# A streaming-encoder layer on one Trainium2 core: the output projection in three phases of block pairs, its weights requested a tile ahead, and the first operands of the up- and down-projection made in the stage before

## The chip, the cores and the metric

The kernel runs on one core of one Trainium2 chip. The core has five instruction queues that work side by side and meet through semaphores: TensorE (PE in the profile, with PEld for its weight loads), VectorE (DVE), ScalarE (ACT), GpSimd (POOL) and SyncE (SP). In this kernel every transfer between the chip's memory (DRAM) and the core's buffer (SBUF) is issued from SP, and 16 DMA engines carry it out. The metric is the device time of one execution in microseconds (us), the median of the runs shown.

## What is computed

The reference is one step of a hybrid encoder layer, cut here to what the change touches. 2048 prompt frames and 64 frames of a running stream are laid side by side as 2112 columns.

```
x = x + mixed @ w_out                    # output projection, 1024 x 1024
xn2 = rmsnorm(x, norm_ffn)
up = xn2 @ w_up                          # 1024 x 5632
up_c, _ = causal_dwconv(up, fbuf, ffn_conv_w, ffn_conv_b)
gate, val = split(up_c, 2)
x = x + (silu(gate) * val) @ w_down      # 2816 x 1024
y = rmsnorm(x, norm_final)
```

Ahead of it lie the input projection, a gated linear recurrence and a windowed attention, which make `mixed`. They aren't changed.

## The kernel before, in words

All activations stand transposed: features on the 128 partitions, frames along the columns. A float32 product is made of three matmuls in a rounded format: an operand is split into a high part (ScalarE, a copy that rounds) and a low part (the difference, on VectorE or GpSimd), and the three are high by high, high by low, low by high. The helper `split` (L188) issues both halves, so that all high parts have line L190 and all low parts L191.

The 2112 columns form three pairs of blocks (`PAIRS`): two blocks of 320, two of 320, two of 416.

**Output projection** (`wout`, L752; matmuls L216 to L218). It runs in four phases: the first pair, the second pair, and the two blocks of 416 as a phase each. A phase goes through eight weight tiles m. In the first phase `kept` loads a tile raw, splits it and stores the split tile of 1 MiB to DRAM (`woS`); the later phases load that (L201), into two buffers. For each tile and block, 24 matmuls fill a PSUM bank, VectorE adds half of the result to the residual (L766), which was loaded from `xT` (L762) into one of two `xres` buffers, the sum is stored to `x1S` (L767), and its square is added to a running sum (L773, L774). Beside the weight tiles a list of generators is driven five steps at a time: `mixes` loads and splits the next phase's input (L754), and `xprep` makes the operands of the up-projection from `x1S` (L722 to L736). Those are seven for each pair: "11", "21", "22" and four sums and differences "T1" to "T4", since the up- and the down-projection multiply by a scheme of seven products instead of eight. After each phase `rms` makes 1/sqrt(mean square) for its blocks (matmul L674, square root L675, reciprocal L676).

**Up-projection** (`Lane`; matmuls L897 to L899). The list `plan` holds steps of one product each. 20 groups of weights serve pair 0 and pair 1 together (two lanes), two groups serve each alone, and then 11 steps with two groups each serve pair 2. Weights are loaded raw (`wraw`), combined (L850), split, and for later use stored to `wuS`. At the first step for pair 1 alone, pair 0's operands are given up and `xprep` begins for pair 2, from `x1S`.

**Down-projection** (matmuls L1191 to L1193). Seven products; in each, every pair goes through 11 weight tiles k, which serve four PSUM banks. `dweight` loads and combines weights (`draw`), four `dw` buffers hold them raw; `dtoken` loads and splits the up-projection's result from `hS`. In the second product a weight tile needs three raw tiles, and the combination is stored to `s2S` (L1117). Finished quarters get their residual and squares (`finished`), and `outputs` scales and stores them.

Memory is handed out by hand: `Region` is a stretch of SBUF, `Pool` gives slots of it by name, in turn, and a slot's next use waits for its last one. `acc` deals out eight PSUM banks in turn. The order on each queue follows the program's text only roughly: a scheduler in the framework places instructions by its own estimates and keeps their dependences. A queue works strictly in order, so what stands behind a waiting instruction waits too.

Of the kernel before, what the change touches and what calls it, by code (L numbers as in the profile page):

```python
# [7 lines left out]
F32 = mybir.dt.float32  # L8
# [43 lines left out]
class Region:  # L52
# [11 lines left out]
    def take(self, n):  # L64
        edges = [(0, 0)] + sorted(self.taken) + [(self.size, self.size)]
        for (_, a), (b, _) in zip(edges, edges[1:]):
            if b - a >= n:
                self.taken.append((a, a + n))
                return self, (a, a + n)
        return None  # L70
# [13 lines left out]
def take(regions, n):  # L84
    n = -(-n // 8) * 8
    for r in regions:
        got = r.take(n)
        if got:
            return got
    raise AssertionError(f"{4 * n} bytes asked for; taken: {[[(4 * a, 4 * b) for a, b in sorted(r.taken)] for r in regions]}")  # L90


class Pool:


    def __init__(self, *regions):
        self.regions, self.slots, self.turn = regions, {}, {}

    def reserve(self, name, n, bufs=1):
        self.slots[name] = [take(self.regions, n) for _ in range(bufs)]  # L100
        self.turn[name] = 0
# [19 lines left out]
def kernel(ctx: ExitStack, tc: tile.TileContext, xT, w_in, w_out, w_up, w_dn, gw, pk,  # L121
# [588 lines left out]

    def xprep(p, names, rs, tp):
# [4 lines left out]
        sums = "T2" in names  # L716
        for k in range(4):
            x = {}
            for o, kk, t in (("11", k, t0), ("12", k, t1), ("21", k + 4, t0), ("22", k + 4, t1)):
                if sums or o in names:  # L720
# [7 lines left out]
            if sums:  # L728
                t2 = tp.tile([P, n], F32, name="xt")
                nc.vector.tensor_tensor(x["11"], x["12"], x["11"], op=ALU.subtract)  # L730
                nc.vector.tensor_tensor(t2, x["22"], x["11"], op=ALU.subtract)
                nc.vector.tensor_tensor(x["12"], x["22"], x["12"], op=ALU.subtract)
                put(p, "T1", k, x["11"])
                put(p, "T2", k, t2)
                yield
                nc.vector.tensor_tensor(t2, x["21"], t2, op=ALU.subtract)  # L736
                put(p, "T3", k, x["12"])
# [3 lines left out]
    wpool, wp2, tp = Pool(RB), Pool(FW), Pool(FW)  # L741
    rawpool = Pool(FW)
    rsum = {}
    phases = [PAIRS[0], PAIRS[1], PAIRS[2][:1], PAIRS[2][1:]]
    mixp = [Pool(RA), Pool(RE), Pool(RE), Pool(RC)]

    def mixes(i):

        for t0, n in phases[i]:
            xblocks[t0] = tuple(mixp[i].tile([P, KO, n], F32R, name=f"{c}{t0}") for c in "hl")  # L750
            hi, lo = xblocks[t0]
            for k in range(KO):  # L752
                mr = wp2.tile([P, BM], F32, name="xk", bufs=2)[:, :n]
                nc.sync.dma_start(mr, mixS[k, :, t0:t0 + n])  # L754
                split(hi[:, k, :n], lo[:, k, :n], mr, nc.gpsimd if k % 3 == 1 and i < 2 else nc.vector)
                yield

    def wout(i, m):
        w = kept(m, i, True)
        for t0, n in phases[i]:  # L760
            xr = wp2.tile([P, BM], F32, name="xres", bufs=2)[:, :n]
# [3 lines left out]
            mm3(ps, w, hi, lo, n)  # L765
            nc.vector.scalar_tensor_tensor(xr, ps[:, :n], 0.5, xr, op0=ALU.mult, op1=ALU.add)  # L766
            nc.sync.dma_start(x1S[m, :, t0:t0 + n], xr)  # L767
            if m == 0:
                rsum[t0] = wp2.tile([P, BM], F32, name="rs", bufs=4)[:, :n]
                nc.scalar.activation(rsum[t0], xr, AF.Square)  # L770
            else:
                q = wp2.tile([P, BM], F32, name="sq", bufs=1)[:, :n]
# [13 lines left out]
    for name, b in (("xk", 2), ("xres", 2), ("rs", 4), ("sq", 1)):  # L786
        wp2.reserve(name, BM, b)
    beside = [mixes(0)]
    drive(beside, 99)
    for i, blocks in enumerate(phases):  # L790
        if i == 1:
            rawpool.close()
            wpool.close()
            wpool = Pool(RE)
            beside.append(xprep(0, ORDER, rsum, tp))
        if i == 2:
            beside.append(xprep(1, ("T1", "T2", "T3", "T4"), rsum, tp))
        if i == 3:
            beside.append(xprep(1, ("11", "21", "22"), rsum, tp))
        if i + 1 < len(phases):  # L800
            beside.insert(0, mixes(i + 1))
        if i == 1:
            wpool.reserve("whl", 2 * KO * P, 2)
        for m in range(8):
            wout(i, m)
            drive(beside, 5)
        drive(beside, 99)
        mixp[i].close()
        for t0, n in blocks:
            rms(rsum[t0], n, rsum[t0])  # L810
            if i > 1:
                nc.sync.dma_start(rS[:, t0:t0 + n], rsum[t0])
    tp.close()
    wp2.close()
    wpool.close()
    RC.close()
    FA = Region(tc, "FA", 26624, F32)
# [3 lines left out]
    wr, wh = Pool(FW), Pool(RE)  # L821

    def wraw(g, o, nb=6):

        t = wr.tile([P, 4 * P], F32, name="wr", bufs=nb)
# [5 lines left out]
    def wops(g, fresh, nh):  # L831
# [3 lines left out]
        def parts(src):  # L835
            t = wh.tile([P, 2, 4 * P], F32R, name="wh", bufs=nh)
# [3 lines left out]
        def kept_s(i, src):  # L840
# [3 lines left out]
            else:  # L844
                t = wh.tile([P, 2, 4 * P], F32R, name="wh", bufs=nh)
# [23 lines left out]
    def flush(i):  # L869
# [5 lines left out]
    class Lane:  # L875
# [48 lines left out]
        def conv_a(self, G, m):  # L924
            self.carry(G, m)
            uc = up["c"].tile([P, self.cols], F32, name="uc", bufs=4)
# [90 lines left out]
    wr.reserve("wr", 4 * P, 6)  # L1017
    up["s"], up["c"] = Pool(FA), Pool(FW, FA)
    up["c"].reserve("uc", 640, 4)
    x2 = []  # L1020

    def prepare(i):
# [3 lines left out]
        for g in dict.fromkeys(g for g, _ in lanes):  # L1026
            if u == 0:
                gens[g] = wops(g, fresh, 4)
# [3 lines left out]
    ahead, made = 3, 0  # L1032
    live = []
    for i, (lanes, fresh, u) in enumerate(plan):
        while made <= i:
            prepare(made)
            made += 1
        if u == 0:
# [312 lines left out]
```

## Time and profile before

| | us |
|---|---|
| median of 3 runs | 3093.64 |
| lowest and highest | 3085.44 and 3097.01 |
| the profiled execution's own time | 3103.43 |
| its span, first to last instruction | 3101.7 |
| PE busy, PEld busy | 2913.0 and 2824.1 |
| DVE, ACT, POOL busy | 2158.4, 1511.6, 168.4 |

The mean granted TensorE clock is 0.967 of full speed. DMA moved 587.06 MB, 189 GB/s over the span. By the first and last matmuls of each line, the input projection with recurrence and attention runs to about 1372 us of the span, the output projection from there to 1662.9, the up-projection to 2607.9 and the down-projection to the end. A row of a group of instructions names its line, engine, operation and tiles (written tile, arrow, read tiles), the shape, the count, busy time and mean duration in ns, and then the idle time ahead of it with what ended that. A row of waits names who waited for whom, the total in us, how often, and the longest. A row by stretches gives, for each engine, its busy us and number of instructions, then the mean granted clock, the mean busy share of the DMA engines and GB/s.

### The profile page before, as it was taken

How to read it: one execution, taken by the hardware profiler on the slowest of the kernel's cores; microseconds unless marked ns; L12 is line 12 of the kernel's file. 1: busy time of each engine (PE TensorE's matmuls, PEld its weight loads, DVE VectorE, ACT ScalarE, POOL GpSimd, SP SyncE). 2: the span in 40 equal slices, each digit the busy share in tenths (PEclk: the TensorE clock that was granted, in tenths of full speed). 3: DMA queues.
4: the chain of work that ended last, by engine and by line, in shares of the span. 5: the costliest groups of instructions: out<-in, count | busy, mean ns of one | idle time of the engine just before them, and what ended most of it. 6: DMA issues, size and time to landing. Idle time of an engine off the chain costs nothing.

```text
span 3101.7 us, 48466 instructions
## 1 busy us (share of the span) xinstructions
PE 2913.0 (94%) x17572; PEld 2824.1 (91%) x17572; DVE 2158.4 (70%) x4176; ACT 1511.6 (49%) x3404; POOL 168.4 (5%) x121
## 2 busy tenths in 40 slices
PE   8999999999999999987878999999799999899997
PEld 7988889999999999976868999999689999899997
DVE  5498882587883588863664888888876677466776
ACT  4576652466561466643323555555444444233442
POOL 3221212000000000002000000000000000000000
PEclk9999999999999999998989999999899999999999
DMA  7865537444336544436775555454776677675764
GB/s 254 284 217 188 182 136 240 154 134 136 126 117 200 165 136 135 137 130 224 253 232 204 176 184 181 164 177 169 265 230 229 227 229 226 196 216 177 223 191 129
DMA packets 338751, 587.06 MB, mean 189 GB/s; under 512 B 34928, under 2 KB 261680, under 8 KB 317520
## 3 DMA queue, kind: packets, MB, share of 16 engines
q1 hardware_dynamic: 338512, 583.97, 57.6%
q8 instruction: 138, 2.26, 0.3%
q14 instruction: 101, 0.83, 0.1%
HBM read 399.19 MB, written 185.18 MB: 188 GB/s over the span
## 4 chain that ended last, share of the span: by engine, by line
PE 43%; DMA 7%; DVE 3%; ACT 1%; issue 1%; SPq 0%; POOL 0%; DVEq 0%; ACTq 0%; POOLq 0%
PE mf L897 6%; PE mf L898 6%; PE mf L899 6%; PE mm L897 3%; PE mm L899 3%; PE mm L898 3%; PE mf L1192 3%; PE mf L1193 3%; PE mf L1191 3%; PE mm L1191 2%; PE mm L1193 2%; PE mm L1192 1%; DMA RE<-woS 1%; DMA FW<-in_w_dn_dram 1%; DMA FW<-mixS 1%; DMA x1S<-FW 1%
## 5 line engine op out<-in xcount | busy, mean ns | idle before, releaser
L216 PE MATMUL mm<-xh,whl 128*128 128x320 f32 (+2 forms) x2112 | 690.5, 327 | 9.7 <-ACT xh L190 6.3
L217 PE MATMUL mm<-xl,whl 128*128 128x320 f32 (+2 forms) x2112 | 688.6, 326 | 8.5 <-DVE xl L191 4.5
L218 PE MATMUL mm<-xh,whl 128*128 128x320 f32 (+2 forms) x2112 | 685.9, 325 | 0.0
L190 ACT ACTIVATE RE<-FW 128x512 fp32r<-128x512 f32 (+2 forms) x586 | 319.2, 562 | 450.3 <-PE mf L1193 74.0
L191 DVE TENSOR_TENSOR RE<-FW,RE 128x512 fp32r<-128x512 f32 (+2 forms) x580 | 345.0, 610 | 162.0 <-ACT RE L190 147.0
L216 PEld LDWEIGHTS mm<-xh,whl 128*128 128x128 f32 x2112 | 402.3, 191 | 17.3 <-ACT xh L190 8.7
L217 PEld LDWEIGHTS mm<-xl,whl 128*128 128x128 f32 x2112 | 401.5, 190 | 17.7 <-DVE xl L191 7.9
L218 PEld LDWEIGHTS mm<-xh,whl 128*128 128x128 f32 x2112 | 401.4, 190 | 0.8
L1192 PE MATMUL mf<-RE 128*128 128x320 f32 (+1 forms) x583 | 190.4, 327 | 5.4 <-DVE RE L191 5.4
L1191 PE MATMUL mf<-RE 128*128 128x320 f32 (+1 forms) x583 | 191.3, 329 | 0.0
L1193 PE MATMUL mf<-RE 128*128 128x320 f32 (+1 forms) x583 | 189.7, 325 | 0.0
L897 PE MATMUL mf<-RE 128*128 128x320 f32 (+1 forms) x472 | 154.8, 330 | 12.2 <-ACT RE L190 9.3
L933 DVE SCALAR_TENSOR_TENSOR FW<-FA,pkt,FW 128x640 f32<-128x640 f32 x176 | 154.7, 879 | 12.0 <-ACT FW L927 8.8
L898 PE MATMUL mf<-RE 128*128 128x320 f32 (+1 forms) x472 | 155.0, 328 | 0.6 <-DVE RE L191 0.6
L899 PE MATMUL mf<-RE 128*128 128x320 f32 (+1 forms) x472 | 154.4, 327 | 0.0
L897 PE MATMUL mm<-RE 128*128 128x320 f32 (+1 forms) x408 | 133.3, 327 | 6.6 <-DMA RE<-wuS 5.7
L897 PE MATMUL mf<-RA,RE 128*128 128x320 f32 (+1 forms) x416 | 137.2, 330 | 0.9 <-ACT FA L944 0.5
L899 PE MATMUL mm<-RE 128*128 128x320 f32 (+1 forms) x408 | 132.1, 324 | 5.4 <-DVE RE L191 5.4
L898 PE MATMUL mf<-RA,RE 128*128 128x320 f32 (+1 forms) x416 | 136.1, 327 | 0.0
L899 PE MATMUL mf<-RA,RE 128*128 128x320 f32 (+1 forms) x416 | 135.9, 327 | 0.2 <-DVE RE L191 0.2
L898 PE MATMUL mm<-RE 128*128 128x320 f32 (+1 forms) x408 | 132.3, 324 | 0.0
L447 ACT ACTIVATE pr<-S,nm 128x256 f32<-128x256 f32 (+1 forms) x272 | 123.3, 472 | 7.6 <-DVE nm L443 6.0
(329 smaller groups left out, 7121.2 us busy)
## 6 DMA issues: line engine op xcount, KB each, us to landing
whl<-wiS SPq DMA_DIRECT2D x88, 1024.0 KB, 5.1
RE<-wuS SPq DMA_DIRECT2D x96, 512.0 KB, 4.4
wiS<-whl SPq DMA_DIRECT2D x44, 1024.0 KB, 4.8
wuS<-RE SPq DMA_DIRECT2D x88, 512.0 KB, 2.7
FW<-in_w_up_dram SPq DMA_DIRECT2D x160, 256.0 KB, 3.4
FW<-in_w_dn_dram SPq DMA_DIRECT2D x121, 256.0 KB, 3.8
hS<-FA SPq DMA_DIRECT2D x154, 160.0 KB, 3.0
FW<-hS SPq DMA_DIRECT2D x154, 160.0 KB, 3.4
```

Source lines behind the costliest of these rows:

```text
L190: nc.scalar.activation(hi, src, AF.Copy)
L191: (lo_eng or nc.vector).tensor_tensor(lo, src, hi.bitcast(F32), op=ALU.subtract)
L216: nc.tensor.matmul(ps[:, :n], wh[:, c], xh[:, k, :n], start=first, stop=False)
L217: nc.tensor.matmul(ps[:, :n], wh[:, c], xl[:, k, :n], start=False, stop=False)
L218: nc.tensor.matmul(ps[:, :n], wl[:, c], xh[:, k, :n], start=False, stop=last)
L897: nc.tensor.matmul(ps[:, :n], w[:, 0, c], x[:, k, 0], start=first, stop=False, **more)
L898: nc.tensor.matmul(ps[:, :n], w[:, 0, c], x[:, k, 1], start=False, stop=False, **more)
L899: nc.tensor.matmul(ps[:, :n], w[:, 1, c], x[:, k, 0], start=False, stop=last, **more)
L933: nc.vector.scalar_tensor_tensor(uc, G[:, j:j + self.cols], col("fw", 44 * j + m), uc, op0=ALU.mult, op1=ALU.add)
L1191: nc.tensor.matmul(ps[m][:, :n], w[:, 0, c], t[:, 0], start=k == 0, stop=False)
L1192: nc.tensor.matmul(ps[m][:, :n], w[:, 0, c], t[:, 1], start=False, stop=False)
L1193: nc.tensor.matmul(ps[m][:, :n], w[:, 1, c], t[:, 0], start=False, stop=k == 10)
```

## The change

The output projection now has three phases, one for each pair. `wout` requests the tile of weights that follows (`wload`) directly behind its own matmuls, ahead of its residual, and the stores of a tile's sums are held in a list and issued one tile later, behind that request. The split weights of the first phase are stored from the same list. Raw weights come in two halves, and all low parts are made on VectorE. Four `xres` buffers stand in place of two. The norm of a phase is made behind the first tile of the next; that of pair 2 only at the first step for pair 1 alone in the up-projection, from sums stored raw in `rS`. `xprep` takes any subset of operands. Pair 0's are made in the second phase, of pair 1 "11", "T3", "T2", "T4" in the third, and "T1", "21", "22" beside the first four steps of the up-projection. The first weights of the up-projection are made within the last tile of the output projection; the first weights and two token tiles of the down-projection within the last four steps of the up-projection. The down-projection's raw weights use six buffers. The adding of residuals is separated from squares and done earlier, and the last product goes through pair 2, pair 1 and then pair 0 twice, with two banks each time.

The SP queue in the stretch of the output projection where blocks of 416 are worked, before (`woS` is the split weights, `x1S` the sums, `xT` the residual):

```order
L201 DMA RE<-woS 128x2048
L762 DMA FW<-in_xT_dram 128x416
L767 DMA x1S<-FW 128x416
L722 DMA FW<-x1S 128x320 x2
L201 DMA RE<-woS 128x2048
L722 DMA FW<-x1S 128x320 x2
L762 DMA FW<-in_xT_dram 128x416
L767 DMA x1S<-FW 128x416
L201 DMA RE<-woS 128x2048
```

and now:

```order
L780 DMA RE<-woS 128x2048
L812 DMA x1S<-FW 128x416
L733 DMA FW<-x1S 128x320 x2
L812 DMA x1S<-FW 128x416
L796 DMA FW<-in_xT_dram 128x416 x2
L733 DMA FW<-x1S 128x320
L780 DMA RE<-woS 128x2048
```

Between two weight tiles stood one residual and one store; now two of each stand there, since a tile serves both blocks.

The VectorE queue at the start of the up-projection, now (L734 scales a loaded tile of `x1S`, L740 forms T1, L198 makes low parts, L866 combines weights; FA is the stretch of memory that holds pair 1's raw tiles):

```order
L734 SCALAR_TENSOR_TENSOR FA<-FA,pkt,FW 128x320 x3
L740 TENSOR_TENSOR FA<-FA 128x320
L198 TENSOR_TENSOR RE<-FW,RE 128x512
L198 TENSOR_TENSOR RE<-FA,RE 128x320 x2
L734 SCALAR_TENSOR_TENSOR FA<-FA,pkt,FW 128x320
L198 TENSOR_TENSOR RE<-FW,RE 128x512
L866 TENSOR_TENSOR FW<-FW 128x512
L734 SCALAR_TENSOR_TENSOR FA<-FA,pkt,FW 128x320 x2
L740 TENSOR_TENSOR FA<-FA 128x320
L734 SCALAR_TENSOR_TENSOR FA<-FA,pkt,FW 128x320
L198 TENSOR_TENSOR RE<-FA,RE 128x320 x2
```

Before, this place held the up-projection's own weights and results alone; the operands of pair 1 had been made in the output projection.

The VectorE queue where pair 1 begins alone, now (FP and FA hold pair 2's sums of squares and raw tiles):

```order
L1008 TENSOR_TENSOR FA<-FA 128x320
L683 RECIPROCAL FP<-FP 128x416
L683 RECIPROCAL FA<-FA 128x416
L734 SCALAR_TENSOR_TENSOR FP<-FP,pkt 128x416
L734 SCALAR_TENSOR_TENSOR FP<-FP,pkt,FA 128x416
```

Before, the first of the scalings stood there without the reciprocals, which ran in the output projection.

The diff, cut to its core:

```diff
+    def wload(i, m):
+        t = wpool.tile([P, 2, KO * P], F32R, name="whl", bufs=2)
+        if i:
+            nc.sync.dma_start(t.bitcast(F32), woS[m])
+        else:
+            for h in range(2):
+                c = slice(h * 4 * P, (h + 1) * 4 * P)
+                raw = raws.tile([P, 4 * P], F32, name="wraw")
+                nc.sync.dma_start(raw, w_out[m][:, c])
+                split(t[:, 0, c], t[:, 1, c], raw)
+            stores.append(lambda: nc.sync.dma_start(woS[m], t.bitcast(F32)))
+        weights[i, m] = t[:, 0], t[:, 1]
...
     def wout(i, m):
-        w = kept(m, i, True)
+        w, work = weights.pop((i, m)), []
         for t0, n in phases[i]:
-            xr = wp2.tile([P, BM], F32, name="xres", bufs=2)[:, :n]
+            xr = io[i].tile([P, n], F32, name="xres")
             nc.sync.dma_start(xr, xT[m * P:(m + 1) * P, t0:t0 + n])
             ps = acc()
             hi, lo = xblocks[t0]
             mm3(ps, w, hi, lo, n)
+            work.append((t0, n, xr, ps))
+        due = stores[:]
+        stores.clear()
+        if m < 7:
+            wload(i, m + 1)
+        for f in due:
+            f()
+        return work
...
-    phases = [PAIRS[0], PAIRS[1], PAIRS[2][:1], PAIRS[2][1:]]
+    phases = [PAIRS[0], PAIRS[1], PAIRS[2]]
...
+        if i == 1:
+            beside = [mixes(2, xk, 2), xprep(0, ORDER, rsum, tp)]
+        if i == 2:
+            beside = [xprep(1, ("11", "T3", "T2", "T4"), rsum, tp)]
+        for m in range(8):
+            work = wout(i, m)
...
+            if i and m == 0:
+                norms(i - 1)
...
+            residual(i, m, work)
+            drive(beside, (2, 4, 2)[i])
...
+    x1, x2 = [xprep(1, (o,), rsum, tp) for o in ("T1", "21", "22")], []
...
+        if u == 0 and x2 and rsum:
+            for t0, n in PAIRS[2]:
+                rms(rs[t0], n, rs[t0])
+            rsum.clear()
...
+        left = len(plan) - 1 - i
+        if left < 4:
+            for _ in range(2 if left else 3):
+                draws(0)
...
-    units = [(i, p) for i in range(7) for p in range(3)]
-    seq = [(i, p, k) for i, p in units for k in range(11)]
+    seq = [(i, p, k, range(4)) for i in range(7) for p in ((0, 1, 2) if i < 6 else (2, 1)) for k in range(11)]
+    seq += [(6, 0, k, r) for r in (range(2), range(2, 4)) for k in range(11)]
...
-        t = dp.tile([P, 4, P], F32, name="dw", bufs=4)
+        t = wr.tile([P, 4, P], F32, name="wr")
```

More of the change, by code (lines that the diff above doesn't have):

```diff
@@ L867, with flush @@
     hold = {}
-    def flush(i):
+    def flush():
         while later:
@@ new lines @@
+    sums[0].reserve("rs", BM, 2)
+    sums[1].reserve("rs", 320, 2)
+    raws.reserve("wraw", 4 * P, 3)
+    xk = Pool(FW)
+    beside = [mixes(0, xk, 6)]
+    drive(beside, 2)
+    wload(0, 0)
+    drive(beside, 99)
+    xk.close()
+    for i in range(3):
+        n = phases[i][0][1]
+        io[i].reserve("xres", n, 4)
+        io[i].reserve("sq", n)
+        xk = Pool(FW)
+        if i == 0:
+            beside = [mixes(1, xk, 2)]
+        if i == 1:
[4 more added lines that the diff above has]
+            work = wout(i, m)
+            if i == 2 and m == 7:
+                drive(beside, 99)
+                tp.close()
+                wr.reserve("wr", 4 * P, 4)
+                made = 0
+            if i and m == 0:
+                norms(i - 1)
+            if i == 2 and m == 7:
+                wpool.close()
+                wh.reserve("wh", 8 * P, 4)
+                for made in (0, 1):
+                    prepare(made)
+                made = 2
+            residual(i, m, work)
+            drive(beside, (2, 4, 2)[i])
+        drive(beside, 99)
+        mixp[i].close()
+        if i == 0:
+            raws.close()
+            wpool.close()
+            wpool = Pool(RE, right=True)
+            wpool.reserve("whl", 2 * KO * P, 2)
+        if i < 2:
+            wload(i + 1, 0)
+            while stores:
+                stores.pop(0)()
+            io[i].close()
+            xk.close()
@@ L1134, with flushing, quarter @@
+    give(2)
+    wh.extend("wh", 8 * P, 5)
+    dr.extend("hh", 2 * BM, 5)
+    def flushing():
+        while later:
+            clock[0] = i = min(later)
+            for f in later.pop(i):
+                f()
+                yield
+    dp = R = None
     ssum = {}
-    def finished(p, q):
+    def quarter(p, q):
         b, n = PAIRS[p][q[1] == "2"]
-        for m in range(4):
-            mm = m + 4 * (q[0] == "2")
+        return b, n, [(m + 4 * (q[0] == "2"), R[p, q][:, m]) for m in range(4)]
@@ L1141, in finished, with resid, squares @@
+    def resid(p, q):
+        b, n, rows = quarter(p, q)
+        for m, y in rows:
             x = dp.tile([P, BM], F32, name="xres", bufs=3)[:, :n]
-            nc.sync.dma_start(x, x1S[mm, :, b:b + n])
-            y = R[p, q][:, m]
+            nc.sync.dma_start(x, x1S[m, :, b:b + n])
             nc.vector.tensor_tensor(y, y, x, op=ALU.add)
+            yield
+    def squares(p, q, ms=range(4)):
+        b, n, rows = quarter(p, q)
+        for m, y in [rows[m] for m in ms]:
             if b not in ssum:
```

343 lines of the change are left out of this document (180 added, 163 removed).

## The prediction

> **What bounds the kernel now.** I read the busy time of the engines by stretches first, cut where the lines of the matmuls change, then TensorE's waits, the chain of waits, and single matmuls. Five stretches matter: the output projection, the point where pair 1 goes on alone and pair 2 begins, the start of the down-projection, and the tail.
>
> ```profile
> 1372.50:1662.90 290.40, 222.21 (x1138) 207.09 (x1139) 137.31 (x263) 80.06 (x162) 21.30 (x16) 0.85 0.73 240
> 2185.00:2260.00 75.00, 53.29 (x261) 49.30 (x261) 64.42 (x111) 32.87 (x67) 0.00 (x0) 0.80 0.78 259
> 2607.90:2730.00 122.10, 105.18 (x618) 103.29 (x618) 64.12 (x115) 41.03 (x91) 0.00 (x0) 0.90 0.68 209
> 3082.30:3101.70 19.40, 2.49 (x6) 0.89 (x5) 12.98 (x20) 2.76 (x5) 0.00 (x0) 0.61 0.28 99
> ```
>
> TensorE idles 68 of 290 us in the output projection, and the granted clock falls to 0.85 there. No engine is full: VectorE has 137 us, DMA 0.73. The waits say whom TensorE waits for:
>
> ```profile
> PE mf L674 <- DVE FW L774: 15.2, 4, 9.0
> PE mm L216 <- DMA RE<-woS: 14.9, 6, 4.4
> PE mf L216 <- ACT RB L190: 11.0, 5, 3.5
> PE mf L216 <- DMA RE<-woS: 9.9, 6, 3.0
> PE mm L1191 <- ACT RE L190: 8.6, 2, 4.9
> PE mf L1192 <- DVE RE L191: 5.4, 1, 5.4
> PE mm L1192 <- DVE RE L191: 3.0, 1, 3.0
> ```
>
> The first four are the output projection: sums for the norm, split weights from DRAM (24.8 us), weights split on the spot. The last three are the down-projection's start. The chain of waits shows why a weight tile comes late:
>
> ```profile
> 1565.10 0.60 DVE FW L766
> 1565.72 5.15 DMA x1S<-FW
> 1570.94 0.33 SPq L762
> ...
> 1572.17 7.30 DMA RE<-woS
> ```
>
> The residual is added, its store needs 5.15 us, the next residual's load waits on SP for that store to free one of two buffers, and the weight load stands behind it. Nothing here is work; it is a queue. What a wait costs beside its length is seen in single matmuls, 320 columns wide after a wait of 2.87 us, then 416 wide:
>
> ```profile
> 1421.14 0.63 PE L216 MATMUL mf<-RA,RB 128*128 128x320 f32 x1 [2.87 <-ACT RB L190]
> ...
> 1423.10 0.47 PE L217 MATMUL mf<-RA,RB 128*128 128x320 f32 x1
> ...
> 1423.90 0.46 PE L217 MATMUL mf<-RA,RB 128*128 128x320 f32 x1
> ...
> 1424.34 0.31 PE L216 MATMUL mf<-RA,RB 128*128 128x320 f32 x1
> ...
> 1426.39 0.31 PE L218 MATMUL mf<-RA,RB 128*128 128x320 f32 x1
> ...
> 1587.93 0.36 PE L217 MATMUL mm<-RE 128*128 128x416 f32 x1
> ...
> 1591.34 0.35 PE L217 MATMUL mm<-RE 128*128 128x416 f32 x1
> ```
>
> From 1423.10 to 1423.90 lie 3 matmuls, 0.27 us each; from 1424.34 to 1426.39 there are 14, 0.146 each; of 416 columns 18 in 3.41 us, 0.189 each. So the array ran at half speed for 3 us after the wait, some 11 matmuls, which is 11 x 0.12 = 1.3 us on top. The stage has 192 matmuls for each of six blocks: 192 x (4 x 0.146 + 2 x 0.189) = 185 us. That is the floor; 290.4 - 185 = 105 us is to be had.
>
> **Output projection, step by step.** The request for tile m+1 now goes out when m starts, ahead of the stores of m-1, and four residual buffers take the store out of the loop. A tile serves two blocks, so the cover for a load is 48 matmuls: 7.0 us in the pairs of 320, 9.1 us in the pair of 416, where one block gave 4.5 us before. The transfers:
>
> ```profile
> RE<-woS SPq DMA_DIRECT2D x23, 1024.0 KB, 6.0
> FW<-x1S SPq DMA_DIRECT2D x44, 160.0 KB, 3.8
> ...
> 1377.00:1382.00 5.00, 3.36 (x14) 2.65 (x13) 0.91 (x2) 0.89 (x2) 0.69 (x1) 0.72 1.00 326
> 1500.00:1520.00 20.00, 15.86 (x107) 15.36 (x105) 16.44 (x39) 7.97 (x18) 0.00 (x0) 1.00 0.86 285
> ```
>
> 6.0 us (7.3 in the chain) hides well in the third phase and barely in the second. Next comes the volume. The stage moves 240 GB/s x 290.4 us = 69.7 MB; eight loads of 1 MiB fall away, and a dozen of the 44 x1S loads move into the next stage (2 MB). By phase, from the sizes in the code's tiles: first 23.0 MB (raw weights 4.2, split weights out 8.4, inputs of two pairs 5.2, residuals and sums 5.2), second 19.6 MB, third about 19 MB. All 16 DMA engines full gave 326 GB/s for 5 us, and 285 is the best that held for 20 us. At 285 the first phase takes 81 us and the second 69, against 56 us of matmuls in each; the third is TensorE's, 8 x 9.1 = 73. With 5 us for the norm between the first two, 228 us. Bounds: at 326 GB/s 71 + 60 + 73 + 5 = 209; at today's 240, 96 + 82 + 79 + 5 = 262. I take 228, since requests are no longer held by single stores, and the 20 us of 285 were just such a stretch: **-62 us** (-28 to -81).
>
> VectorE takes over GpSimd's 21 us of low parts, and loses two reciprocals and some scalings. Its rows:
>
> ```profile
> L723 DVE SCALAR_TENSOR_TENSOR FW<-FW,pkt 128x320 f32<-128x320 f32 x44 | 22.4, 543 | 8.2 <-DMA FW<-x1S 8.1
> L191 DVE TENSOR_TENSOR RE<-FW,RE 128x320 fp32r<-128x320 f32 x38 | 20.8, 572 | 11.7 <-ACT RE L190 11.2 <-PE mf L218 0.4
> L676 DVE RECIPROCAL FW<-FW 128x416 f32<-128x416 f32 x1 | 2.8, 2753 | 0.8 <-ACT FW L675 0.8
> L850 DVE TENSOR_TENSOR FW<-FW 128x512 f32<-128x512 f32 x88 | 60.1, 683 | 2.4 <-DMA FW<-in_w_up_dram 1.7
> ```
>
> 16 half tiles of weights at 0.68 are 11 us where three whole ones stood (4), a dozen more low parts 6, first weights of the up-projection 4, minus 12 scalings (6.5) and 2.8: 137 + 7 + 6 + 4 - 6.5 - 2.8 = 145 us, 64% of 228. It is covered, but in the second phase, where all of pair 0's operands are made, it is nearly full; without the cover a tile there would take 11 us instead of 7.
>
> The Trainium skill, page "TensorE: Matmul & The Clock Gate", section "What's actually happening", says that the array goes to half clock after about an idle window of 3.4 us. By that, the short waits that I leave in the second phase would cost no clock. The row above shows half speed after 2.87 us; by it, eight such waits would cost 10 us, and the measurement decides.
>
> **Start of the up-projection.** T1, 21 and 22 of pair 1 are made there: 16 loads, 16 scalings, 4 subtractions, 12 low parts. Each raw tile has one buffer, so that they come in four rounds: load 3.8, then two scalings, one subtraction and a low part of about half a us each, 2.1 us, then the next load. Four rounds end after 24 us, and the stage's own weight splits in the same queue add some 3. T1's last quarter is needed about 20 us after the start (the queue puts it behind six of seven products, each 24 x 0.146 = 3.5 us). So TensorE is late by some 6 us, and the present stage has a few waits there already: **+5** (0 to 12).
>
> **Pair 1 alone.** Two reciprocals of 2.75 us come ahead of pair 2's first scalings, in a stretch where VectorE is busy 64.4 of 75 us, and two matmuls wait for rS there, with the following products queued behind them. The DMA latency lies beside the reciprocals' delay: **+5.5** (0 to 11).
>
> **Start of the down-projection.** The second product's weights are late, by this chain:
>
> ```profile
> 2646.33 4.11 DMA FW<-in_w_dn_dram
> 2650.47 0.70 DVE FW L1115
> 2651.19 0.70 DVE FW L1116
> 2651.91 3.08 DMA s2S<-FW
> ```
>
> 8.7 us for each weight tile with four buffers for three raw tiles: 11 take 95 us, where 11 steps of pair 1 and 11 of pair 2 and the following pair 0 give 19 + 25 + 18 = 62. Six buffers hold two sets, so that two chains overlap: about 4.5 us each, 50 us in all. That takes away 8.6 + 3.0 us; the 5.4 at the first product shrinks, since its tokens and weights come earlier. With the half speed behind three waits (4), at most 21; I take **-13** (-3 to -20), as the last results of the up-projection still share VectorE.
>
> **Tail.**
>
> ```profile
> L1160 DVE SCALAR_TENSOR_TENSOR RR<-RR,pkt,FD 128x416 f32<-128x416 f32 x8 | 4.6, 647 | 0.0
> L676 DVE RECIPROCAL FD<-FD 128x416 f32<-128x416 f32 x1 | 2.8, 2752 | 2.5 <-ACT FD L675 2.5
> L1151 DVE TENSOR_TENSOR FD<-FD 128x416 f32<-128x416 f32 x4 | 2.4, 590 | 0.9 <-ACT FD L1150 0.7
> L1144 DVE TENSOR_TENSOR RR<-RR,FW 128x416 f32<-128x416 f32 x4 | 2.2, 582 | 0.0
> ```
>
> The residuals (2.2) are added before; two banks instead of four leave half of the squares' sums (1.2) and of the last additions (1.1); 320 columns instead of 416 save a quarter of the rest (1.7): **-6** (-4 to -8). Pair 0's 11 tokens are loaded and split twice, 11 x 0.57 = 6 us of VectorE under 19 us of matmuls: **+1** (0 to 4).
>
> Sum: -62 + 5 + 5.5 - 13 - 6 + 1 = -69.5. The profiled execution took 3103.4, so 3034 for its like; it lies 9.8 above the median 3093.6, so **3024 us** in the runs' terms.
>
> **Rivals.** First, transfers keep today's pace: 240 GB/s, as stores and loads still meet in one queue. The output projection takes 262, the net is -35: 3058. For it: 0.73 is the mean over the stage; against it: the gaps coincide with waits on single stores. Second, it hides better: 326 GB/s held, the floor almost reached, 209 us, and the start of the down-projection free (-20): net -95, 2999. The Trainium skill, "DMA: Bandwidth & Descriptors", section "Where 436 GB/s comes from", gives about 358 GB/s for one core from the memory side; no row here is above the 326 at full share for 5 us. Third, the change doesn't do what it says: loads of weights still stand behind stores that wait for VectorE, so that the 24.8 us of waits stay, and only the shape of the phases pays, -20, with the added 11.5 and the tail: about 3080. Fourth, slower: VectorE's queue sets the pace. In the output projection it is now busy 137 of 290 us, 47%, mostly between ScalarE's half and its own. If that share stays, 145 us of work need 308 us, +18; the rounds at the up-projection's start go the same way (+12), reciprocals +5.5, and -18 from the rest: +17, 3111. It decides where the share stays under 50%; against it, the share was higher where this kind of work was densest:
>
> ```profile
> 1475.00:1560.00 85.00, 67.58 (x420) 64.70 (x419) 52.33 (x109) 29.26 (x62) 0.00 (x0) 0.90 0.76 245
> ```
>
> 52.33 of 85 us are 62%, which gives 234.
>
> **How the numbers follow.** Forecast 0.58, the first rival 0.18, the second 0.12, the third 0.06, the fourth 0.06. About 0.5%, 15 us, can be told from no change. Faster by more: the first three, 0.87; within: 0.07 (most of the third); slower: 0.06. The range holds the forecast, the first rival and most of the second: 2990 to 3064; the likeliest one's own is 3005 to 3045.
>
> **What would show it.** Right: the output projection in 220 to 235 us at 265 GB/s or more, no wait on RE<-woS above 1 us in the third phase; a wait of 3 to 10 us at the first T1 of pair 1; SP's chain over s2S gone. Wrong: DMA share still 0.73 (first rival), or VectorE under 50% with TensorE waiting for L198 (fourth).

## The result

| | before | changed |
|---|---|---|
| median us (runs) | 3095.3 (4) | 3022.3 (4) |
| lowest, highest | 3085.4, 3097.1 | 3020.9, 3027.7 |
| profiled execution, its span | 3103.4, 3101.7 | 3023.8, 3022.0 |

The ratio of the means is 0.977 (95% interval 0.975 to 0.980). The forecast was 3024. The number came out; the reason given for its largest term did not, as the runs below show.

First the stretches of the changed kernel: the three phases of the output projection, pair 0 and pair 1 alone, the first 122 us of the down-projection, its last 23 us, and the tail.

```profile
1373.10:1449.10 76.00, 64.60 (x388) 59.68 (x388) 42.07 (x82) 31.87 (x64) 0.00 (x0) 0.92 0.92 316
1449.10:1519.50 70.40, 62.06 (x384) 61.33 (x385) 41.00 (x89) 23.77 (x51) 0.00 (x0) 0.92 0.78 261
1519.50:1600.00 80.50, 76.28 (x391) 73.83 (x390) 51.28 (x102) 22.94 (x46) 0.00 (x0) 0.98 0.72 238
...
2109.60:2181.50 71.90, 45.56 (x244) 40.19 (x244) 64.10 (x106) 35.99 (x70) 0.00 (x0) 0.85 0.79 265
...
2541.00:2663.00 122.00, 116.99 (x716) 112.40 (x715) 77.39 (x142) 47.61 (x102) 0.00 (x0) 1.00 0.83 251
...
2987.00:3010.00 23.00, 16.17 (x89) 14.98 (x87) 16.79 (x35) 5.01 (x13) 0.00 (x0) 0.78 0.58 193
...
3009.60:3022.00 12.40, 1.01 (x4) 0.30 (x2) 7.66 (x13) 1.47 (x3) 0.00 (x0) 0.64 0.31 106
```

The kernel before, cut in the same way for the output projection (its third and fourth phase together in the third row) and for pairs 0 and 1 alone:

```profile
1372.50:1470.80 98.30, 70.36 (x340) 63.89 (x341) 29.79 (x51) 27.37 (x52) 19.60 (x16) 0.79 0.71 236
1470.80:1559.50 88.70, 70.16 (x438) 67.22 (x437) 54.29 (x113) 30.61 (x65) 1.71 (x1) 0.91 0.76 245
1559.50:1668.80 109.30, 86.93 (x390) 80.92 (x389) 55.11 (x104) 22.63 (x46) 0.00 (x0) 0.87 0.71 235
...
2181.50:2249.50 68.00, 46.18 (x240) 42.37 (x240) 58.28 (x103) 32.00 (x66) 0.00 (x0) 0.83 0.80 264
```

The last tile of the output projection ran after 1662.9, where the prediction had cut; the stage ended at 1668.8 and took 296.3 us, so it lost 69 us, not 63. From there to pair 2's first product the time went from 580.9 to 581.8 us, from there to the down-projection from 359.0 to 359.6, the down-projection to its last matmul from 474.2 to 468.4, and what lies behind it from 19.0 to 12.5. With the 0.6 us by which the stage began later the sum is -79.7, the difference between the two profiled executions.

TensorE's waits in the changed output projection, in order of total:

```profile
PE mf L223 <- DMA RE<-woS: 12.3, 6, 4.2
PE mm L223 <- DMA RE<-woS: 3.9, 2, 3.7
PE mf L681 <- DVE FW L819: 2.8, 1, 2.8
PE mf L225 <- DVE RB L198: 1.8, 3, 1.5
```

Waits for weights from DRAM fell from 24.8 to 16.2 us, the norm's from 15.2 to 2.8, and those for weights split on the spot (the rows of RB) from 25.5 to 4.8.

### The profile page after: what moved, and what is told of

Read it like the earlier page. It is cut to its first block, busy times and chain, and to the rows that moved or that the text cites. A ratio compares the mean times of both kernels' runs of the same rounds, so it can differ in the third digit from the quotient of the medians.

```text
span 3022.0 us, 48591 instructions
## 1 busy us (share of the span) xinstructions
PE 2883.6 (95%) x17572; PEld 2797.1 (93%) x17572; DVE 2173.0 (72%) x4220; ACT 1520.8 (50%) x3427; POOL 146.2 (5%) x104
## 4 chain that ended last, share of the span: by engine, by line
PE 70%; DVE 11%; DMA 9%; ACT 3%; issue 2%; SPq 1%; POOL 0%; DVEq 0%; ACTq 0%; POOLq 0%
PE mm L224 8%; PE mm L223 8%; PE mm L225 8%; PE mf L913 6%; PE mf L914 6%; PE mf L915 6%; PE mm L913 4%; PE mm L915 4%; PE mm L914 4%; PE mf L1306 2%; PE mf L1307 2%; PE mf L1305 2%; PE pt L467 1%; PE mm L1306 1%; PE mm L1307 1%
## 5 line engine op out<-in xcount | busy, mean ns | idle before, releaser
L198 DVE TENSOR_TENSOR RE<-FW,RE 128x512 fp32r<-128x512 f32 (+2 forms) x585 | 344.4, 604 | 182.6 <-ACT RE L197 164.7
L223 PEld LDWEIGHTS mm<-xh,whl 128*128 128x128 f32 x2112 | 401.1, 190 | 16.2 <-ACT xh L197 8.0
L1307 PE MATMUL mf<-RE 128*128 128x320 f32 (+1 forms) x594 | 191.0, 322 | 0.0
L913 PE MATMUL mf<-RE 128*128 128x320 f32 (+1 forms) x472 | 155.0, 330 | 19.3 <-ACT RE L197 15.1
```

Of the source, the lines that this page charges most:

```text
L198: (lo_eng or nc.vector).tensor_tensor(lo, src, hi.bitcast(F32), op=ALU.subtract)
L223: nc.tensor.matmul(ps[:, :n], wh[:, c], xh[:, k, :n], start=first, stop=False)
L913: nc.tensor.matmul(ps[:, :n], w[:, 0, c], x[:, k, 0], start=first, stop=False, **more)
L1307: nc.tensor.matmul(ps[m][:, :n], w[:, 1, c], t[:, 0], start=False, stop=k == 10)
```

## Experiments on the output projection

Up to this stage all kernels here are the same code, and yet it began between 1364 and 1376 us of the span. So stretches are compared, from matmul to matmul. "First two" runs from the stage's first matmul to the first of 416 columns (in some kernels a tile of the second phase is placed ahead of the first phase's last, so the two are not parted), "third" from there to the last. The five kernels whose first two phases are those of the change needed 142.7 to 148.7 us for them; this is the noise of one profile. Each ratio below is against executions of the kernel before made alongside, whose medians were 3089 to 3095 us; medians of two rows can differ by some 6 us for that alone. The rows of whole raw tiles, of single blocks and of 10.5 MB more are one execution each.

| kernel | first two, us | third, us | median us |
|---|---|---|---|
| before | 187.0 | 109.3 | 3095 |
| changed | 146.4 | 80.4 | 3022 |
| changed, old order of requests | 150.3 | 81.2 | 3027 |
| before, requests a tile ahead | 181.0 | 103.8 | 3089 |
| changed, whole raw tiles and GpSimd | 144.4 | 79.3 | 3017 |
| changed, both of these undone | 164.8 | 82.5 | 3047 |
| changed, third phase by single blocks | 146.7 | 100.5 | 3041 |
| changed, 10.5 MB more in the first phase | 167.3 | 80.9 | 3033 |
| changed, weights from GpSimd's queue | 130.5 | 93.2 | 3023 |

### The order of requests, undone and done alone

```diff
 def wout(i, m):
+    if m:
+        wload(i, m)
...
-    if m < 7:
-        wload(i, m + 1)
...
 def residual(i, m, work):
...
-    stores.append(lambda ...: nc.sync.dma_start(x1S[m, :, t0:t0 + n], xr))
+    nc.sync.dma_start(x1S[m, :, t0:t0 + n], xr)
...
-io[i].reserve("xres", n, 4)
+io[i].reserve("xres", n, 2)
```

> The changed kernel with its three phases of pairs, but in them the order of requests from before: each split weight tile is asked for when its own tile starts, residual stores go out as soon as they are made, and there are two residual buffers instead of four. The prediction's theory (a request that stands behind a single store was what made the tiles late): most of the 69 us come back, the output projection takes 226.9 + 30 to + 45, that is 257 to 272 us, TensorE's waits on RE<-woS rise from 16 us to over 35. Rival (the shape of the phases alone, two blocks for each weight tile, brings the gain): the output projection stays under 235 us and the waits under 22 us.

In the kernel before, the other way round (`kept(m + 1, i, True)` called behind tile m's first residual load):

> The kernel before with one edit: in its four phases each weight tile is asked for while the tile before it is worked on, right after that tile's first residual load; two residual buffers and stores at once stay as they were. If asking earlier is enough, the 24.8 us of waits on RE<-woS fall below 12 us and the output projection from 296 us (to its last matmul) to about 280. Rival (the request cannot go earlier, since the buffer of the tile before is freed only when that tile's matmuls end, and then the stores are there already; without held stores and more residual buffers nothing moves): waits on RE<-woS 20 to 28 us, output projection 292 to 300, total within 8 us of before.

The first took 3027 us, ratio 0.979 (0.977 to 0.982): the output projection 231.5 us, waits on RE<-woS 15.5. The rival was right, and the prediction's reason fell: the order of requests is worth some 5 us here, hardly more than the noise, and not the bulk. Its stretches:

```profile
1367.30:1444.70 77.40, 64.96 (x387) 61.44 (x387) 40.23 (x80) 30.54 (x62) 0.00 (x0) 0.91 0.90 309
1444.70:1517.60 72.90, 63.82 (x386) 62.96 (x387) 49.51 (x106) 27.97 (x60) 0.00 (x0) 0.89 0.79 264
1517.60:1598.80 81.20, 76.27 (x390) 73.46 (x389) 44.87 (x86) 17.55 (x37) 0.00 (x0) 0.98 0.67 219
```

The second gave 0.999 (0.9975 to 1.0006) of before; waits on RE<-woS were 20 us, and the stage, 285 us in its profile, lay between the two expectations. Asking earlier by itself gains nothing that the runs can tell.

### Two blocks for each weight tile

```diff
+passes = [(m, phases[i]) for m in range(8)]
+if i == 2:
+    passes = [(m, (b,)) for b in phases[2] for m in range(8)]
-for m in range(8):
-    work = wout(i, m)
+for j, (m, blocks) in enumerate(passes):
+    work = wout(i, m, blocks)
...
-    drive(beside, (2, 4, 2)[i])
+    drive(beside, (2, 4, 1)[i])
```

> The changed kernel with one edit: in the third phase the two blocks of 416 columns are worked one after the other, as before the change, each with its own eight weight loads; the order of requests (a tile ahead, held stores, four residual buffers) stays. The run with the old order of requests has shown that this order is worth under 5 us; so the cover must be what counts. Theory now (a load of 7.3 us is covered by the 9.1 us of two blocks and not by the 4.6 us of one): the third phase goes from 80.4 to 100 to 110 us, near the 109 of before, with 15 us or more of waits on RE<-woS. Rival (asked for a tile ahead, a load is covered also by one block, since two buffers let it start while the tile before runs): under 90 us.

The third phase took 100.5 us instead of 80.4, with 14.2 us of waits on RE<-woS in eleven pieces (changed kernel: 4.2):

```profile
1519.80:1620.30 100.50, 81.97 (x391) 75.77 (x390) 53.44 (x102) 23.05 (x46) 0.00 (x0) 0.95 0.81 272
```
```profile
PE mf L223 <- DMA RE<-woS: 7.6, 6, 2.1
PE mm L223 <- DMA RE<-woS: 6.6, 5, 2.1
```

So 20 of the 29 us of the third phase come from the pairing, with the new order of requests in place. Pairing gives each load twice the matmuls to hide under and drops eight loads of 1 MiB; the run undoes both at once. A wait of 5.2 us for the norm between the two blocks went with the change too.

### The first phase: weights split on the spot

```diff
-    for h in range(2):
-        c = slice(h * 4 * P, (h + 1) * 4 * P)
-        raw = raws.tile([P, 4 * P], F32, name="wraw")
-        nc.sync.dma_start(raw, w_out[m][:, c])
-        split(t[:, 0, c], t[:, 1, c], raw)
+    raw = raws.tile([P, KO * P], F32, name="wraw")
+    nc.sync.dma_start(raw, w_out[m])
+    turn[0] += 1
+    split(t[:, 0], t[:, 1], raw, nc.gpsimd if turn[0] % 3 else nc.vector)
...
-raws.reserve("wraw", 4 * P, 3)
+raws.reserve("wraw", KO * P, 1)
```

> The changed kernel with one edit: in the first phase the raw weights come as before the change, one whole tile in one buffer, with the low part on GpSimd for two of three (before: load 3.9 us, ScalarE 1.06, GpSimd 2.36, so at least 7.3 us for each tile against 7.0 us of matmuls, and the next load only after that); requests stay a tile ahead. Theory (this chain, and not the line of stores, made the first phase slow): the stretch to the second phase's first tile goes from 76 us back to 88 to 98 (before 98), with 15 us or more of waits on RB. Rival (a tile ahead is enough cover for a chain of 7.3 us): under 80 us.

It cost nothing: 144.4 us for the first two phases. The theory fell again. Then this edit and the old order of requests together:

> The changed kernel with both earlier edits together: the old order of requests (each tile asked for at its own start, stores at once, two residual buffers) and whole raw tiles in one buffer with two of three low parts on GpSimd. Each edit alone left the stretch to the second phase at 74 to 77 us. Theory (each of the two changes alone takes the wait for split weights out of the first phase; only without both does a tile's chain of load 3.9, ScalarE 1.06, GpSimd 2.36 us start too late): the stretch goes to 92 to 104 us, near the 98 of before, with over 15 us of waits on RB. Rival (something else speeds up the first phase, for instance that one tile of the second phase's weights and mixes no longer share its queue): under 82 us, and the 30 us that before loses there stay unexplained by these two.

The first two phases took 164.8 us, 18 us more, where the edits alone had cost 4 and -2; total 3047, ratio 0.986 (0.983 to 0.989). Its first two rows, and the waits of its first phase:

```profile
1373.90:1457.10 83.20, 62.48 (x341) 58.43 (x342) 34.03 (x57) 25.59 (x51) 10.16 (x5) 0.86 0.79 270
1457.10:1538.70 81.60, 70.92 (x433) 69.15 (x433) 54.53 (x111) 30.41 (x64) 1.68 (x1) 0.92 0.74 243
```
```profile
PE mf L223 <- ACT RB L197: 11.9, 5, 6.2
PE mf L225 <- POOL RB L198: 4.0, 3, 1.6
PE mm L223 <- ACT RB L197: 3.4, 1, 3.4
```

The waits on RB are back (19.3 us in these rows), though the stretch to the second phase's tile is 83, not 92 to 104. Over the first two phases all waits on RB together are 25.5 us in the kernel before, 4.8 in the changed one, 9.1 with the old order alone, 7.0 with whole raw tiles alone and 22.3 with both. So the new order of requests and the new handling of raw tiles (halves in three buffers, low parts on VectorE) stand in for each other: either one hides most of the chain of load, high part and low part. Of the 41 us that the first two phases lost, these two explain 18. The norm behind the next phase's first tile accounts for about 7 by the waits (9.5 us on L674 there before, 2.8 on L681 now) and some half speed; that was not run by itself, and some 15 us stay unexplained. Waits for the first pair's own inputs (RA) are part of them: they fell from 6.0 to 1.3 us, and the change loads these inputs through six buffers instead of two, which no run undoes.

### Are the transfers the pace of the first phase?

```diff
+spare = dram.tile([8, P, KO * 320], F32, name="spare")
...
+    if i == 0:
+        nc.sync.dma_start(spare[m], xblocks[0][0].bitcast(F32).rearrange("p k n -> p (k n)"))
     due = stores[:]
```

> The changed kernel, which in each of the eight tiles of the first phase also stores one block's high and low parts' first half (1.31 MB, ready long before) to a spare tensor in DRAM: 10.5 MB more on the same queue. If the transfers set the first phase's pace (share 0.93, 320 GB/s), it takes 10.5 MB / 320 GB/s = 33 us longer: 66.8 + 33 = 100 us at the same 310 to 325 GB/s. Rival (the pace is set by splits and TensorE, 58 us of matmuls, and the share is high by chance): under 80 us, and a rate above 360 GB/s.

To the first phase's last matmul, the changed kernel and this one:

```profile
1373.10:1440.00 66.90, 62.00 (x384) 58.73 (x384) 36.26 (x74) 27.98 (x57) 0.00 (x0) 0.95 0.93 320
```
```profile
1364.30:1448.00 83.70, 67.84 (x384) 63.91 (x384) 36.65 (x76) 27.36 (x57) 0.00 (x0) 0.88 1.00 377
```

Neither side: 17 us more, at 377 GB/s. With 0.93 of the engines busy the phase was close to what the transfers allow but not on it, and the rate at full share is no constant.

### Weight loads out of SP's line

In the second phase, the chain of waits of the changed kernel shows a residual load in SP's queue right ahead of a weight load that is late:

```profile
1475.66 0.43 SPq L796
1476.14 7.50 DMA RE<-woS
1483.77 0.40 PE mf L223
```

```diff
-    nc.sync.dma_start(t.bitcast(F32), woS[m])
+    nc.gpsimd.dma_start(t.bitcast(F32), woS[m])
```

> The changed kernel with one edit: in the second and third phase the split weight tiles are loaded from GpSimd's queue, which has nothing else to do there, instead of SP's. Theory (what is left of the waits on RE<-woS, 16 us with 4 to 5 us of half speed, comes from requests that stand in SP's line behind loads of residuals and of the next pair's inputs, which wait for buffers): waits under 5 us, the two phases 70.4 + 80.5 = 151 us fall by 10 to 16 us, the total to 3008 to 3014. Rival (the weight transfers themselves are slow, 7.5 to 8.4 us, because the engines are shared with other loads): waits stay above 12 us, the total within 5 us of 3022.

The waits went as the theory had it (RE<-woS 0.4 us in the two phases, the first two phases 16 us shorter), and the total stayed, 0.9775 (0.975 to 0.980). TensorE reaches the norm of pair 1 sooner, and VectorE has not yet made its sum:

```profile
PE mf L681 <- DVE FW L819: 15.9, 2, 15.0
PE mf L223 <- DMA RE<-woS: 0.4, 1, 0.4
```

In those 15 us VectorE idles for little more than 2:

```profile
1512.30:1527.30 15.00, 0.03 (x1) 0.00 (x0) 12.70 (x32) 6.16 (x14) 0.53 (x1) 0.63 0.58 197
```

This is the prediction's fourth rival, VectorE's queue as the pace, one step further on: it decides once the weights are on time.

## Experiments on the later stages

### Raw buffers at the down-projection's start

```diff
 give(2)
+old, t = wr.slots["wr"], wr.turn["wr"] % len(wr.slots["wr"])
+wr.slots["wr"], wr.turn["wr"] = (old[t:] + old[:t])[:4], 0
```

> The changed kernel with one edit: when the up-projection is through, the raw down-projection weights get four buffers instead of six, as before the change. Theory of the prediction (with four, one chain of load, two subtractions and store, 8.7 us, can be under way at a time, and the second product's weights are late): waits of about 8.6 + 3.0 us at the second product come back, with half speed behind them +11 to +15 us in the first 120 us of the down-projection, total 3033 to 3037. Rival (the chain is short enough since the first product's weights are now made before the up-projection ends, so that the second product's start earlier): within 4 us of 3022.

3035.5 us, ratio 0.981 (0.976 to 0.985); the down-projection took 483.5 us instead of 468.4. As the theory had it, the waits came back at the second product (L1307 and L1308 are its matmuls here):

```profile
PE mm L1307 <- ACT RE L197: 10.2, 3, 5.0
PE mm L1308 <- DVE RE L198: 3.5, 2, 2.0
```

### Pair 0's tokens twice

The last half of the last product in the changed kernel, on VectorE:

```profile
2981.77 2.75 DVE L683 RECIPROCAL FD<-FD 128x416 f32<-128x416 f32 x1
...
2984.78 4.58 DVE L1286 SCALAR_TENSOR_TENSOR RR<-RR,pkt,FD 128x416 f32<-128x416 f32 x8
2989.28 2.15 DVE L683 RECIPROCAL FD<-FD 128x320 f32<-128x320 f32 x1
2991.34 0.43 DVE L198 TENSOR_TENSOR RE<-FW,RE 128x320 fp32r<-128x320 f32 x1
```

```diff
 def fetch(j):
...
+    if ms[-1] == 3 and ms[0]:
+        toks[j] = toks_held[k]
+        return
     toks[j] = dtoken(prods[i][1], p, k)
+    if len(ms) == 2:
+        toks_held[k] = toks[j]
...
+if (i, p, k) == (6, 2, 0):
+    ...
+    dr.slots["hh"], dr.turn["hh"] = free + old[t:] + old[:t], 0
```

> The changed kernel with one edit: in the last product the 11 split token tiles of pair 0 stay in their buffers (eleven instead of seven, four from weight tiles that are free by then), so that the second half reads them again and neither loads nor splits them a second time. Theory (the two waits of 4.5 and 2.1 us in the second half are tokens whose low part stands in VectorE's queue behind 12 us of reciprocals and outputs of other blocks): both waits go, with about 1.5 us of half speed, total 3013 to 3016. Rival (VectorE's batch only moves, and the tail waits for it instead): the waits go, the stretch behind the last matmul grows from 12.4 us by as much, total within 3 us of 3022.

Both waits went, the tail stayed at 12.7 us against 12.5, and the down-projection fell from 468.4 to 456.0: 3011 us, ratio 0.972 (0.969 to 0.976). Its last 23 us, with 152 matmuls at full clock where the changed kernel has 89 at 0.78:

```profile
2976.00:2999.00 23.00, 22.95 (x152) 22.18 (x150) 19.17 (x34) 4.66 (x10) 0.00 (x0) 1.00 0.37 132
```

63 matmuls of 0.146 us are 9 us; the waits are 6.6 of them, the rest is half speed.

### Pair 2's norm

```diff
-if u == 0 and x2 and rsum:
-    for t0, n in PAIRS[2]:
-        rms(rs[t0], n, rs[t0])
-    rsum.clear()
+if i == 60:
+    for t0, n in PAIRS[2]:
+        rsum[t0] = up["u"].tile([P, 640], F32, name="uc")[:, :n]
+        nc.sync.dma_start(rsum[t0], rS[:, t0:t0 + n])
+if i == 62:
+    for t0, n in PAIRS[2]:
+        rms(rsum[t0], n, rsum[t0])
+        nc.sync.dma_start(rS[:, t0:t0 + n], rsum[t0])
```

> The changed kernel with one edit: the norm of pair 2 (two reciprocals of 2.75 us) is worked out in the middle of the up-projection, from the sums in DRAM and back, not where pair 1 goes on alone. Theory (the prediction's term of +5.5, which the trace puts at 71.95 - 67.95 = +4 us): the stretch from pair 1's first product alone to pair 2's first product falls from 72 to 67 or 68 us, the wait of 9.6 us at pair 2's first product to about 6, total 3016 to 3019. Rival (pair 2's loads, in four rounds, end last anyway): stretch 70 to 72 us, total within 2 us of 3022.

Pair 2's first product in the changed kernel, and in this one:

```profile
2181.56 1.06 PE L913 MATMUL mf<-RE 128*128 128x416 f32 x2 [9.64 <-ACT RE L197]
```
```profile
2164.29 0.65 PE L913 MATMUL mf<-RE 128*128 128x416 f32 x2 [2.81 <-ACT RE L197]
```

From the first wait of pair 0 alone (2109.61 and 2101.26) these are 72.0 and 63.0 us; before it was 68.0. The stretch shrank by 9, more than the theory's 4 to 5 and more than the two reciprocals of 2.75 us. VectorE was busy 64.1 of 72 us there and is busy 58.6 of 63 now: 5.5 us of the 9 are the reciprocals' work, the rest is not explained. 3008.5 us, ratio 0.972 (0.969 to 0.976), also beyond the theory; of the 22 us that its profiled execution gained, 14 lie in stages that the edit does not touch.

### All of it together

The kept tokens, the early norm and the weights from GpSimd's queue, and two edits more: the norm of the second pair behind the third tile of the third phase, and pair 1's operands after it.

```diff
-if i and m == 0:
+if (i, m) in ((1, 0), (2, 2)):
     norms(i - 1)
...
-drive(beside, (2, 4, 2)[i])
+drive(beside, (2, 4, 3 if m > 1 else 0)[i])
```

> The changed kernel with the edits of the runs with kept tokens, with the early norm of pair 2 and with weight loads from GpSimd's queue, and one more: the second pair's norm stands behind the third phase's third tile instead of its first, so that TensorE does not stand 15 us in front of a sum that VectorE has yet to make; the preparation of pair 1 starts after it. Theory (parts add up): -12 in the down-projection, -7 to -12 in the up-projection, output projection from 227 to 205 to 212 us, total 2983 to 2993. Rival (VectorE's queue sets the pace of the second and third phase together, so that the wait only moves, for instance to the start of the up-projection): output projection and start of the up-projection together gain under 6 us, total 2996 to 3004.

The output projection took 204.4 us, as expected, and then TensorE stood for 20 us at the start of the up-projection:

```profile
1530.00:1574.90 44.90, 44.90 (x239) 44.30 (x237) 22.43 (x41) 8.38 (x18) 1.58 (x3) 1.00 0.63 207
1574.90:1600.00 25.10, 4.67 (x17) 4.29 (x17) 19.44 (x40) 7.36 (x16) 0.00 (x0) 0.55 0.51 166
```
```profile
PE mf L913 <- ACT RE L197: 22.7, 2, 20.4
```

3005.8 us, ratio 0.971 (0.969 to 0.974). The wait moved, as the rival said, but not because VectorE is full: it idles half of the 45 us ahead, and waits for pair 1's loads of x1S, which stand in SP's line. From 1530 to 1600 us of the span SP itself stands 35.2 us in front of residual loads (L796) that wait for a store to free their buffer:

```profile
1564.41 0.55 DVE L734 SCALAR_TENSOR_TENSOR FW<-FW,pkt 128x320 f32<-128x320 f32 x1 [8.67 <-DMA FW<-x1S]
```

So these loads went to GpSimd's queue as well, and the operands were driven by four steps for each tile instead of three:

```diff
-nc.sync.dma_start(x[o], x1S[kk, :, t:t + n])
+(nc.gpsimd if p == 1 and len(names) > 1 else nc.sync).dma_start(x[o], x1S[kk, :, t:t + n])
...
-drive(beside, (2, 4, 3 if m > 1 else 0)[i])
+drive(beside, (2, 4, 4 if m > 1 else 0)[i])
```

> The changed kernel with kept tokens, early norm of pair 2, weight loads of the second and third phase from GpSimd's queue, the second pair's norm behind the third phase's third tile, as in the run before, and one more edit: the loads of x1S for pair 1's operands in the third phase also come from GpSimd's queue. Theory (the 20.4 us wait at the up-projection's start came from these loads, which stood in SP's line behind residual loads that wait for buffers, so VectorE idled 22 of 45 us): the wait falls under 5 us, output projection 203 to 208 us, total 2985 to 2992. Rival (the loads on GpSimd's queue wait there for VectorE's tiles and hold the weights up instead): waits on RE<-woS over 8 us in the third phase or still over 10 us at the start of the up-projection, total 2996 to 3008.

The rival again, a little beyond its own range: 3011.7 us, 0.975 (0.973 to 0.976), with a wait of 19.1 us for weights. On GpSimd's queue a load of x1S waits 27 us for VectorE, and the weight load stands behind it:

```profile
1494.85 0.53 POOL L780 DMA_DIRECT2D RE<-woS  x1 [6.51 <-DMA FW<-in_xT_dram]
1522.69 1.08 POOL L733 DMA_DIRECT2D FW<-x1S  x2 [27.32 <-DVE RB L198]
1523.76 0.54 POOL L780 DMA_DIRECT2D RE<-woS  x1
```

The kernels with kept tokens, with the early norm, and with all but the last edit beat both the kernel before and the changed one: every execution of theirs is shorter than each of the changed kernel's, though the intervals of the first two still touch its own. They cannot be told from each other by their intervals. The first two alone, together, were not run.

## Why the prediction was right, and where it was not

**The total came out to 2 us by luck.** Between the two profiled executions the change took off 79.7 us, where the sum said 69.5: the output projection gave 69 and not 62, since the prediction had cut the stage 6 us short, the start of the up-projection -3 and not +5, and pair 0's tokens cost about 9 and not 1. The forecast was met because it then took off the 9.8 us by which the profiled execution of before lies above its median, while that of the changed kernel lies 1.4 above its own.

**What bounds the kernel: the diagnosis was wrong.** "Nothing here is work; it is a queue" is the step that failed, and with it "four residual buffers take the store out of the loop". The chain of waits of before did show a store, a residual load and a weight load in a row, but going back to that order costs 5 us, and the change did not end it. SP still stands in front of residual loads that wait for a store to free a buffer, before (L762) and now (L796), as these rows of SP's own waits over the output projection say:

```profile
SPq L762 <- DMA x1S<-FW: 44.2, 25, 5.9
SPq L796 <- DMA x1S<-FW: 39.8, 18, 5.0
```

What fell is SP's time in front of stores whose sums VectorE had not added yet (53.6 us before, 16.6 now). The 69 us of TensorE's time are the pairing in the third phase (20 by its run), the first phase's weights (18 by the run with both edits undone), the norm moved behind a tile (about 12 by the waits, 15.2 against 2.8), and a rest of 19 that no run parts. One chain that ended last does not say what else would have ended a little earlier.

**The term of -62 held by errors that cancel.** First phase: 66.8 us instead of 81, since it moved 21.4 MB, not 23.0, at 320 GB/s; 285 had been the best 20 us of a stage at a share of 0.86, and so not what the transfers allow. Norm between: 9.2 us instead of 5, where the next weight load is late as well. Second: 70.4 against 69. Third: 80.5 against 73; it was not TensorE's alone, with waits of 4.2 us on RE<-woS, the longest 3.4, where none above 1 us was to be seen. With those waits under 1 us, in the run with all of it together, it took 74.1.

**Start of the up-projection, +5: about -3.** From the stage's first matmul to pairs 0 and 1 alone it took 513.0 us before and 509.8 now. The four rounds did end some 24 us after the start; the 3 us that the stage's own splits were to add did not show. TensorE waited for T1's third quarter, and used the last one only at 23.6 us, since a product of pair 0 had been placed in between:

```profile
1617.86 0.42 PE L913 MATMUL mf<-RE 128*128 128x320 f32 x1 [1.03 <-ACT RE L197]
1618.69 0.42 PE L914 MATMUL mf<-RE 128*128 128x320 f32 x1 [0.41 <-DVE RE L198]
...
1623.56 0.42 PE L913 MATMUL mf<-RE 128*128 128x320 f32 x1
```

That is 1.4 us, where the kernel before waited 2.5 us in the first 60 us of the stage. The step that failed is the due time of T1's last quarter, set at 20 us.

**Pair 1 alone, +5.5: +4**, and of the right kind: without the reciprocals there the stretch is 9 us shorter, more than the term.

**Start of the down-projection, -13: -14.** In its first 122 us there are 716 matmuls where there were 618, 98 x 0.146 = 14 us; TensorE's waits there fell from 17.0 to 4.5 us, and four buffers bring 15 us of time back.

**Pair 0's tokens twice, +1: about +9**, the term most in error for its size. Six us of VectorE "under 19 us of matmuls" left out what else stands in that queue in those 19 us, in order: two reciprocals and eight outputs, 9.5 us, ahead of one token's low part, and eight more outputs, 3.8 us, ahead of the next.

**Tail, -6: -6.5.**

**What a wait costs beside its length** is not the same each time. In the kernel before, matmuls of 320 columns ran 0.27 us apart behind the prediction's wait of 2.87 us and behind one of 2.42 us at 1397.34, but 0.146 us apart at once behind waits of 2.50 us at 1504.04 and 2.19 us at 1520.54. So 1.3 us for each wait is no fixed price.

**The rivals.** The share of the DMA engines was 0.81 and not 0.73, so the first did not come, nor did the third, though its mechanism, loads of weights behind other requests in SP's line, is what is left of the waits. The second needed 209 us for the output projection; it took 226.9, at 271 GB/s and not 326. VectorE's busy time was 134 us in 226.9, 59%; the fourth needed under 50%.

## What to carry to other kernels

A chain of waits names what ended last, not what a cure is worth: undo the suspected cause by itself before building on it, and undo two changes together when each alone costs nothing, since either may cover for the other. Work that is moved under a stretch of matmuls has to be laid beside everything in its engine's queue for that stretch, in order, not beside its idle share. When one wait is removed, look up which engine the next instruction in TensorE's order needs; here the same 15 to 20 us turned up in a norm, at the next stage's start and in weights, one after another.

## What was not expected of the hardware

With long stores added, all 16 DMA engines moved 377 GB/s over 84 us, in this stretch of the same run 389:

```profile
1440.00:1456.00 16.00, 9.22 (x53) 7.73 (x53) 9.04 (x14) 5.73 (x11) 0.00 (x0) 0.87 1.03 389
```

In the kernel before a share of 1.00 had meant 326 GB/s. The added stores have rows of 10,240 bytes, the loads of inputs rows of 1,280; that the row's length makes the difference was not tried by itself. The Trainium skill, page "DMA: Bandwidth & Descriptors", section "Where 436 GB/s comes from", puts the limit of the memory side at about 358 GB/s for a core, half of what a stack gives to two. The 377 here, with one core at work, are above that, and the measurement decides. GpSimd takes twice as long as VectorE for the low part of a whole weight tile, as groups of the first phase of before show, and giving two of three tiles back to it, in the one execution with whole raw tiles, cost no time:

```profile
L191 POOL TENSOR_TENSOR RB<-FW,RB 128x1024 fp32r<-128x1024 f32 x5 | 11.8, 2360 | 31.8 <-ACT RB L190 27.8 <-DMA FW<-in_xT_dram 4.0
...
L191 DVE TENSOR_TENSOR RB<-FW,RB 128x1024 fp32r<-128x1024 f32 x3 | 3.7, 1223 | 1.9 <-ACT RB L190 1.9
```
